# The short-convolution half of an output projection as block products, placed inside the SSD half

## The chip, the core and the metric

One NeuronCore of a Trainium2 chip runs one launch of the kernel. The metric is the device time of that launch in microseconds. PE is the matrix engine TensorE, DVE the vector engine, ACT the scalar engine, POOL GpSimd, and SP the sync engine, whose queue issues most transfers. SBUF is the on-chip memory, PSUM the accumulators that PE writes.

## The reference, cut to what matters

One layer of a hybrid decoder runs on 1024 prompt tokens and 8 x 8 sample tokens (1088 tokens in all, 1024 channels, float32). One input projection feeds a short gated convolution and a Mamba-2 scan (SSD). Both results, side by side, go through one output projection:

```python
h = rmsnorm(x, g_mix_pre) * (1 + scale_m) + shift_m
proj = h @ w_in
u = sc_c * sc_x
uc, new_sc_buf = causal_dwconv(u, sc_buf, sc_conv_w)
y_sc = sc_b * uc                       # 1024 channels
...
y_ssd = rmsnorm(yg, 1.0).reshape(bsz, L, SSM_WIDTH) * ssm_norm_g   # 1024 channels
mix = jnp.concatenate([y_sc, y_ssd], axis=-1) @ w_out              # 2048 x 1024
x = x + gate_m * rmsnorm(mix, g_mix_post)
h2 = rmsnorm(x, g_ffn_pre) * (1 + scale_f) + shift_f
f = (jax.nn.silu(h2 @ w_gate) * (h2 @ w_up)) @ w_down
x = x + gate_f * rmsnorm(f, g_ffn_post)
```

The change concerns the product of `y_sc` with the first 1024 rows of `w_out`, the "short-convolution half"; the product of `y_ssd` with the other 1024 rows is the "SSD half".

## The kernel before, in words

**Arithmetic.** A float32 value is held as a high part (`hi`, a cast on ACT) and a low part (`lo`, the difference, on DVE). A product of two such values is three matmuls: weight high with data high, weight high with data low, weight low with data high. In *plain* form (`acc3`, L343 to L345) a tile of 128 output channels takes 8 blocks of 128 input channels x 3 = 24 matmuls per chunk of tokens. The chunks `OC` of the output projection are 512, 304 and 272 tokens wide.

**Block products.** Much of the kernel uses a 2x2x2 scheme with seven products in place of eight (`unit`, L1085 on). Input channels, output channels and tokens are each cut in two. `combos_w` makes seven sums of weight blocks, `sums_h` seven of data blocks (the *factors*); each product p multiplies one with the other. A unit is two tiles of output channels over all 1088 tokens: for each product in the order 1, 5, 6, 3, 7, 2, 4 (`ORDER`) and for each token half q, 4 blocks x 3 = 12 matmuls of 272 columns (`product`, L1087 to L1089). A unit therefore has 7 x 2 x 12 = 168 matmuls, gathered in PSUM banks of the pools `pm` and `pz`, four banks each. After each product ACT copies the bank to its place or DVE adds it there.

**The short convolution's stage** (about 505 to 766 us) comes last in the mixer's input part. For each of 4 pairs of channel tiles there are three units (`sc_unit`), the convolution and the gating product. The pair's result `y_sc` is split whole (`split`, casts at L307) and written by SP to `y_d[0..7]` in device memory (L958, L959). `y_d[8..15]` hold the SSD result.

**The output projection** (from 765.72) has weights two tiles of output channels at a time (`load_cols`: raw transfer, cast L320, low half L321), two buffers of each part. First the SSD half: 8 tiles x 3 chunks, copied from PSUM into the accumulator `acc` by ACT. Then the short-convolution half plain: chunk 0 for all 8 tiles, chunk 1, and chunk 2, each added by DVE (L1330). Within chunk 1, at tiles 0, 2 and 5, stand the steps of `mix_tail` for tokens 0 to 511: transposes of `acc` back to rows (L1248), their scaling and statistics (L1250, L1255), an inverse root from short DVE operations (L282 to L294), the row update (L1265), and the second norm's statistics. After two tiles of chunk 2 the scaled rows (L1357, ACT) are transposed (L1365) as operands of the feed-forward part. The rest of chunk 2 is interleaved with that part's start.

**What sets the order.** A recording layer lays down each engine's instructions; `in_order` pins a piece behind the last recorded matmul, so in these stages PE runs tiles in the order of the code, and each engine works through its own queue in order.

## Time and profile before

| | |
|---|---|
| time, three runs | 1719.84, 1723.9, 1725.52 us (median 1723.9) |
| profiled execution | 1722.96 us, its span 1721.3 us, mean granted PE clock 0.992 |
| busy: PE, DVE, ACT, POOL | 97%, 67%, 45%, 11% of the span |
| last unit of the short convolution | 744.69 to 765.72 us |
| output projection up to the transposes at L1365 | 765.72 to 946.66 us |
| PE waits in 765 to 947 us | two: 2.3 us and 1.0 us |
| moved by transfers over the execution | 256.37 MB, mean 149 GB/s |

In a row of a timeline stand the start, the time from the start to the end, engine, line, operation, output and inputs, shapes, and in brackets the engine's idle time before it with what ended that. Consecutive matmuls overlap, so their distance from start to start is their pace, and their "busy" time is longer than that. In a row of windows stand the window, its busy time of PE, of PE's weight loads, DVE, ACT and POOL with counts, then the granted PE clock, the share of the transfer engines in use and GB/s.

### The profile page before, as it was taken

The numbers are of one execution on the slowest core, as the hardware profiler recorded it, in microseconds if no ns is written. First come the engines' busy times: TensorE is split into PE (matmuls) and PEld (weight loads), VectorE is DVE, ScalarE is ACT, GpSimd is POOL, SyncE is SP. The second block draws the span as 40 slices with busy tenths as digits, with TensorE's granted clock in tenths as the row PEclk, the third lists the DMA queues.
The fourth block names the chain that finished last, engine by engine and source line by source line (L and its number), as shares of the span: only waits on it lengthen the run. The fifth ranks groups of instructions, "written<-read, shape, count | busy, mean of one in ns | idle before, by whom it ended". The sixth has DMA issues, their size and how long they took to land. (4 is left out here: it accounts for less than half of the span.)

```text
span 1721.3 us, 31266 instructions
## 1 busy us (share of the span) xinstructions
PE 1676.9 (97%) x12604; PEld 1595.7 (93%) x12604; DVE 1145.5 (67%) x2190; ACT 772.1 (45%) x1575; POOL 185.5 (11%) x271
## 2 busy tenths in 40 slices
PE   5999999999999999999999999999999999999997
PEld 4898888899999999998989999999999999999987
DVE  5588777777798776661037879666665658688734
ACT  3447454557444433322226776444444446422222
POOL 2110101000001000000000000122222200022112
PEclk9999999999999999999999999999999999999999
DMA  9301344442412522348285634334434338865523
GB/s 318 79 13 38 120 147 155 150 127 77 131 48 79 176 83 62 114 164 305 69 257 184 196 135 147 115 141 142 145 135 141 140 117 314 320 244 197 201 92 139
DMA packets 159623, 256.37 MB, mean 149 GB/s; under 512 B 10577, under 2 KB 123393, under 8 KB 157942
## 3 DMA queue, kind: packets, MB, share of 16 engines
q1 hardware_dynamic: 159190, 253.19, 43.3%
q8 instruction: 99, 1.62, 0.4%
q10 hardware_dynamic: 288, 1.18, 0.2%
q14 instruction: 46, 0.38, 0.1%
HBM read 184.63 MB, written 69.71 MB: 148 GB/s over the span
## 5 line engine op out<-in xcount | busy, mean ns | idle before, releaser
L321 DVE TENSOR_TENSOR wl<-raw,wh 128x512 fp32r<-128x512 f32 (+1 forms) x87 | 61.2, 730 | 101.2 <-ACT wh L320 87.0
L343 PE MATMUL pm<-h,wh 128*128 128x384 f32 (+1 forms) x342 | 114.3, 334 | 0.0
L344 PE MATMUL pm<-h,wh 128*128 128x384 f32 (+1 forms) x342 | 114.0, 333 | 0.0
L345 PE MATMUL pm<-h,wl 128*128 128x384 f32 (+1 forms) x342 | 113.6, 333 | 0.0
L345 PE MATMUL pm<-hb,wl 128*128 128x512 f32 (+2 forms) x320 | 107.6, 338 | 2.3 <-DVE wl L321 2.3
L344 PE MATMUL pm<-hb,wh 128*128 128x512 f32 (+2 forms) x320 | 107.6, 337 | 0.0
L320 ACT CAST wh<-raw 128x512 fp32r<-128x512 f32 (+1 forms) x89 | 56.4, 666 | 114.0 <-PE pm L344 66.4
L343 PE MATMUL pm<-hb,wh 128*128 128x512 f32 (+2 forms) x320 | 105.6, 337 | 1.0 <-ACT wh L320 1.0
L1048 ACT CAST wd<-raw 128x256 fp32r<-128x256 f32 x112 | 42.9, 406 | 90.5 <-PE pz L1089 33.7
L345 PEld LDWEIGHTS pm<-hb,wl 128*128 128x128 f32 x320 | 60.9, 190 | 7.8 <-DVE wl L321 2.5
L1049 DVE TENSOR_TENSOR fs<-f,fs 128x576 fp32r<-128x576 f32 (+2 forms) x76 | 52.5, 705 | 21.6 <-ACT fs L1048 20.8
L343 PEld LDWEIGHTS pm<-hb,wh 128*128 128x128 f32 x320 | 60.6, 191 | 6.7 <-ACT wh L320 1.2
L343 PEld LDWEIGHTS pm<-h,wh 128*128 128x128 f32 x342 | 65.0, 190 | 1.5 <-issue 0.9
L344 PEld LDWEIGHTS pm<-h,wh 128*128 128x128 f32 x342 | 65.0, 190 | 1.2 <-issue 0.7
L1089 PE MATMUL pz<-fc,wd 128*128 128x288 f32 x224 | 66.2, 295 | 0.0
L1087 PE MATMUL pz<-fc,wd 128*128 128x288 f32 x224 | 66.2, 295 | 0.0
L1088 PE MATMUL pz<-fc,wd 128*128 128x288 f32 x224 | 66.1, 295 | 0.0
L345 PEld LDWEIGHTS pm<-h,wl 128*128 128x128 f32 x342 | 64.9, 190 | 1.2 <-issue 1.0
L344 PEld LDWEIGHTS pm<-hb,wh 128*128 128x128 f32 x320 | 60.8, 190 | 5.2
L1089 PE MATMUL pm<-fc,wd 128*128 128x256 f32 x224 | 63.2, 282 | 0.0
L1087 PE MATMUL pm<-fc,wd 128*128 128x256 f32 x224 | 63.1, 282 | 0.0
L1088 PE MATMUL pm<-fc,wd 128*128 128x256 f32 x224 | 62.9, 281 | 0.0
(5573 smaller groups left out, 6196.7 us busy)
## 6 DMA issues: line engine op xcount, KB each, us to landing
raw<-in_w_in SPq DMA_DIRECT2D x48, 512.0 KB
wa<-in_w_ada SPq DMA_DIRECT2D x32, 512.0 KB
raw<-in_w_out SPq DMA_DIRECT2D x32, 512.0 KB
f_d<-fs SPq DMA_DIRECT2D x28, 576.0 KB
f_d<-fs SPq DMA_DIRECT2D x30, 512.0 KB
raw<-in_w_gate SPq DMA_DIRECT2D x28, 512.0 KB
raw<-in_w_up SPq DMA_DIRECT2D x28, 512.0 KB
y_d<-y SPq DMA_DIRECT2D x26, 544.0 KB
```

The source lines that it names most:

```text
L320: (nc.gpsimd.tensor_copy if hi_eng else nc.scalar.copy)(wh, raw)
L321: (eng or nc.vector).tensor_tensor(wl, raw, wh, op=sub)
L343: mm(ps[:, :n], wh, xh, start=(first and j == 0), stop=False)
L344: mm(ps[:, :n], wh, xl, start=False, stop=False)
L345: mm(ps[:, :n], wl, xh, start=False, stop=(last and j == end))
L1048: nc.scalar.copy(hi, v)
L1049: (eng or nc.vector).tensor_tensor(lo, v, hi, op=sub)
L1087: mm(ps, W[0][k], X[0][k], start=(start and k == 0), stop=False, skip_group_check=True)
L1088: mm(ps, W[0][k], X[1][k], start=False, stop=False, skip_group_check=True)
L1089: mm(ps, W[1][k], X[0][k], start=False, stop=(stop and k == nk - 1), skip_group_check=True)
```

## The change

The short-convolution half of the output projection becomes four units of seven products over all 1088 tokens: 672 matmuls of 272 columns in place of 576 of 512, 304 and 272. The order of the stage is now: SSD half chunk 0 (opens the accumulator of the first 512 tokens, by ACT copies), the four units (their block that crosses token 512 is added on one side of it and opens the accumulator on the other, `acc_blocks`), SSD half chunk 1 with the tail of tokens 0 to 511, a small state output that stood earlier, SSD half chunk 2.

`y_sc` is no longer split and written whole. `factors` makes the seven data factors of a pair, by four DVE subtractions in place and a cast and a low half each. For the first three pairs that happens during the next pair's units, one step per product (`puts`): make a factor in the one buffer of the pool `psx`, then at the next step write it to `yx_d` with a transfer that ACT's queue issues. The last pair's factors are made during SSD chunk 0 and stay in SBUF, but for 2 and 4, which go through device memory. During chunk 0 SP's queue loads the others back; factors 2 and 4 of all pairs come last, into the slots of chunk 0's operands.

The SSD weights are now prepared by `plain_w` in eight slots, two pairs of tiles ahead, and the units' weights by `combos_w` in the same slots.

```diff
-    y_d = [drp.tile([P, 2, T], F32, tag=f"y_d{k}", name=f"y_d{k}") for k in range(16)]
+    y_d = [drp.tile([P, 2, T], F32, tag=f"y_d{k}", name=f"y_d{k}") for k in range(8)]
+    yx_d = [[drp.tile([P, 2, T // 2], F32, tag=f"yx_d{g}{p}", name=f"yx_d{g}_{p}") for p in range(1, 8)] for g in range(4)]
...
+    def factors(y, put):
+        (b11, b12), (b21, b22) = blocks_h(y[0]), blocks_h(y[1])
+        yield from put(1, b11)
+        yield from put(2, b21)
+        yield from put(3, b22)
+        nc.vector.tensor_tensor(b11, b12, b11, op=sub)
+        yield from put(5, b11)
+        nc.vector.tensor_tensor(b12, b22, b12, op=sub)
+        yield from put(7, b12)
+        nc.vector.tensor_tensor(b22, b22, b11, op=sub)
+        yield from put(6, b22)
+        nc.vector.tensor_tensor(b21, b21, b22, op=sub)
+        yield from put(4, b21)
+    def factor_parts(t, b):
+        t = t.bitcast(F32R).rearrange("p (s q n) -> p s q n", s=2, q=2)
+        part(t[:, 0], t[:, 1], b)
+    def put_sc(pr):
+        def put(p, b):
+            t = yt(psx)
+            factor_parts(t, b)
+            yield
+            nc.scalar.dma_start(yx_d[pr][p - 1].rearrange("p s n -> p (s n)"), t)
+            yield
+        return put
...
         for m in range(2):
-            y, hi, lo = cc[m], ext[m][:, :T].bitcast(F32R), cb[m].bitcast(F32R)
-            nc.vector.tensor_tensor(y, y, cb[m], op=mult)
-            split(hi, lo, y)
-            kept.append((2 * pr + m, hi, lo))
+            nc.vector.tensor_tensor(cc[m], cc[m], cb[m], op=mult)
         if pr < 3:
-            while kept:
-                y_out(*kept.pop(0))
+            puts = factors(cc, put_sc(pr))
...
-    rawp, wp = pool(left, "rawo", 4), pool(left, "wo", 2)
-    fa, fx, fb = pool(left, "fa", 4), pool(left, "fx", 8), pool(left, "fb", 7)
+    rawo, wo, fa = pool(left, "rawo", 4), pool(left, "wo", 4), pool(left, "fa", 4)
+    fx, fb = pool(left, "fx", 8), pool(left, "fb", 7)
+    raw_from, w_from = [rawo] * 4, [wo] * 4 + [fa] * 4
...
+    last = factors(y_last, put_last)
+    loads_ = (((1, 0), (1, 1), (1, 2), (5, 0), (5, 1), (5, 2)), ((6, 0), (6, 1), (6, 2)),
+              ((7, 0), (7, 1), (3, 0), (3, 1)), ((3, 2), (7, 2)))
+    for mp in range(4):
+        ws = out_load(mp)
+        load_factors(*loads_[mp])
...
+        for m in range(2):
+            in_order(out_tile, 0, terms0, ws[m], 2 * mp + m, True)
+            if mp < 2:
+                in_order(next, last, None)
+                in_order(next, last, None)
+    run(last)
+    load_factors(*((p, pr) for p in (2, 4) for pr in range(4)))
...
+    for mp in range(4):
+        W = combos_w(w_out, 0, nc.vector, raws_of.pop(0))
...
+        unit(W, X_o, 4, [0, 1], acc_blocks(mp), True, {}, SQ)
...
-    out_proj(0, terms[0], {0: [nxt], 2: [nxt]}, out_load)
-    tail = mix_tail([0, 1, 2, 3], lambda t: load_x(t, fb, "fm"), rows_fm, G_m)
+    terms = {c: out_split(c) for c in (1, 2)}
+    tail = mix_tail([0, 1, 2, 3], lambda t: load_x(t, fx, "fm"), rows_fm, G_m)
     out_proj(1, terms[1], {0: [tail], 2: [tail], 5: [tail]}, out_load)
+    in_order(conv_state, nsc, 8, 2, o["scc_p"], o["scc_s"], lambda: fx.tile([P, D], F32, tag="fm", name=nm("cs")))
     out_proj(2, terms[2], {1: [tail], 2: [tail]}, out_load, (0, 1))
```

Lines shift by two in the helpers: what was L343 to L345 is L345 to L347, L1087 to L1089 is L1089 to L1091, L1049 is L1051.

PE where the short-convolution half begins. Before, the last plain tile of the SSD half (272 columns) is followed by that half's chunk 0 (`hb` is a data operand, `wh` and `wl` the weight's parts):

```order
L343 MATMUL pm_975_8944<-hb_923_8229,wh_968_8808 128x272
L344 MATMUL pm_975_8944<-hb_924_8230,wh_968_8808 128x272
L345 MATMUL pm_975_8944<-hb_923_8229,wl_969_8809 128x272
L343 MATMUL pm_992_9006<-hb_978_8974,wh_988_8994 128x512
L344 MATMUL pm_992_9006<-hb_978_8974,wh_988_8994 128x512
L345 MATMUL pm_992_9006<-hb_978_8974,wl_989_8995 128x512
```

After, the last tile of the SSD half's chunk 0 is followed by product 1 of the first unit (`yx` is a factor read back):

```order
L345 MATMUL pm_995_8630<-hb_941_8325,wp__989_8593 128x512
L346 MATMUL pm_995_8630<-hb_941_8325,wp__989_8593 128x512
L347 MATMUL pm_995_8630<-hb_941_8325,wp__989_8593 128x512
L1089 MATMUL pm_1013_8701<-yx_948_8341,w1__1004_8672 128x272
L1090 MATMUL pm_1013_8701<-yx_948_8341,w1__1004_8672 128x272
L1091 MATMUL pm_1013_8701<-yx_948_8341,w1__1004_8672 128x272
```

Where the plain half had 24 groups (8 tiles in 3 chunks) of 24 matmuls, there are 28 products of 24 matmuls (two token halves of 12).

ACT's queue in the third pair of the short convolution, before (`w5` to `w7` are weight factors, the copies empty PSUM, L307 is the whole split):

```order
L1102 COPY y_840_7266<-pm_850_7296 128x272
L307 CAST y_837_7239<-y_797_6771 128x1088
L1102 COPY y_840_7266<-pz_851_7310 128x272
L1048 CAST w2__866_7517<-raw_861_7500 128x512
L1102 COPY y_856_7494<-pm_869_7527 128x272
L307 CAST y_838_7252<-y_798_6772 128x1088
L1102 COPY y_856_7494<-pz_870_7541 128x272
```

After, in the last pair, which makes the third's factors (128x544) and issues their writes:

```order
L1050 CAST y_892_7788<-y_804_6807 128x544
L1234 DMA yx_d2_5_134<-y_892_7788 128x1088
L1050 CAST w2__899_7810<-raw_894_7793 128x512
L1106 COPY y_871_7555<-pm_883_7587 128x272
L1050 CAST y_906_7878<-y_804_6807 128x544
L1106 COPY y_871_7555<-pz_884_7601 128x272
L1050 CAST w3__900_7814<-raw_894_7793 128x512
L1234 DMA yx_d2_7_136<-y_906_7878 128x1088
L1106 COPY y_872_7556<-pm_902_7820 128x272
```

Casts of half the width with their writes stand between the copies; the second cast shown uses the buffer that the first write reads.

DVE behind the row update in chunk 1, before (`wl_1076` and `wl_1078` are the low halves of the weights of tiles 6 and 7 of the same chunk, used by `pm_1079` and `pm_1080`):

```order
L1265 SCALAR_TENSOR_TENSOR x_1040_9338<-y_1044_9343,sm_1062_9471,x_1040_9338 128x1024
L1330 TENSOR_TENSOR acc1_8210<-acc1_8210,pm_1070_9538 128x304
L1330 TENSOR_TENSOR acc1_8210<-acc1_8210,pm_1071_9564 128x304
L321 TENSOR_TENSOR wl_1076_9612<-raw_1073_9607,wh_1075_9611 128x512
L321 TENSOR_TENSOR wl_1076_9612<-raw_1074_9609,wh_1075_9611 128x512
L282 TENSOR_SCALAR sm_1072_9590<-ssn_285 128x4
L321 TENSOR_TENSOR wl_1078_9618<-raw_1073_9607,wh_1077_9617 128x512
```

After (`wp__1130` and the two behind it belong to the first tiles of chunk 2, used by `pm_1134` and `pm_1135`):

```order
L1294 SCALAR_TENSOR_TENSOR x_1086_9632<-y_1090_9637,sm_1106_9761,x_1086_9632 128x1024
L1354 TENSOR_TENSOR acc1_8298<-acc1_8298,pm_1114_9828 128x304
L1354 TENSOR_TENSOR acc1_8298<-acc1_8298,pm_1115_9854 128x304
L1051 TENSOR_TENSOR wp__1130_9984<-raw_1128_9980,wp__1130_9984 128x512
L284 TENSOR_SCALAR sm_1116_9880<-ssn_305 128x4
L1051 TENSOR_TENSOR wp__1131_9987<-raw_1129_9982,wp__1131_9987 128x512
L291 TENSOR_SCALAR sm_1116_9880<-sm_1116_9880 128x4
L1051 TENSOR_TENSOR wp__1132_9990<-raw_1128_9980,wp__1132_9990 128x512
```

The weights' low halves at this place are those of a later pair of tiles. From the row update to the last of the short operations (L294, then L296) ten such low halves stand before, seven after.

More of the change, by code (lines that the diff above doesn't have):

```diff
@@ L1100, in unit @@
                 queue(product, ps, W[p], X[q][p], nk, new, p in (3, 2, 4))
-                if first and opens:
-                    nc.scalar.copy(out(q, i, h), ps)
-                else:
-                    nc.vector.tensor_tensor(out(q, i, h), out(q, i, h), ps, op=add)
+                to = out(q, i, h)
+                for v, cols, opening in to if isinstance(to, list) else [(to, slice(0, blocks_[q][1]), first)]:
+                    if opening and opens:
+                        nc.scalar.copy(v, ps[:, cols])
+                    else:
+                        nc.vector.tensor_tensor(v, v, ps[:, cols], op=add)
             for gen in between.get(n, ()):
@@ L1329, in out_tile, with out_load @@
         v = acc_at(m, c0, n)
-        nc.vector.tensor_tensor(v, v, ps[:, :n], op=add)
+        if opens:
+            nc.scalar.copy(v, ps[:, :n])
+        else:
+            nc.vector.tensor_tensor(v, v, ps[:, :n], op=add)
+    def out_load(mp):
+        W = plain_w(w_ssd, 256 * mp, raws_ahead.pop(0) if raws_ahead else None)
+        return [[[W[m, j][e][k] for j in range(2) for k in range(4)] for e in range(2)] for m in range(2)]
+    raws_ahead = [raws_plain(0), raws_plain(1)]
+    terms0 = out_split(0)
@@ new lines, in hymba_step, with x_tile, load_factors, put_last @@
+    staged = {p: yt(yp4) for p in (2, 4)}
+    x_tiles = {}
+    def x_tile(p, pr):
+        pl = {1: btp, 5: h2p, 6: fb, 3: yp4, 7: yp2 if pr == 2 else fb, 2: fx, 4: fx}[p]
+        t = x_tiles[p, pr] = yt(pl) if pl in (yp4, yp2) else pl.tile(
+            [P, T], F32, tag="bt" if pl is btp else "fm", name=nm("yx"))
+        return t
+    def load_factors(*which):
+        for p, pr in which:
+            nc.sync.dma_start(x_tile(p, pr), yx_d[pr][p - 1].rearrange("p s n -> p (s n)"))
+    def put_last(p, b):
+        t = staged[p] if p in staged else x_tile(p, 3)
+        factor_parts(t, b)
+        if p in staged:
+            nc.sync.dma_start(yx_d[3][p - 1].rearrange("p s n -> p (s n)"), t)
+        yield
@@ L1411, in out_load2 @@
     def out_load2(mp):
-        raws = [raw_half(w_out, j, 256 * mp) for j in range(2)]
+        raws = [raw_half(w_ssd, j, 256 * mp) for j in range(2)]
         out = []
```

83 lines of the change are left out of this document (41 added, 42 removed).

## The prediction

> **What bounds the kernel now.** I read the page's busy shares, its clock row and its chain of waits first, then where TensorE (PE) waited in the two stages the change touches, and last the timeline of each wait.
>
> ```profile
> span 1721.3 us, 31266 instructions
> PE 1676.9 (97%) x12604; PEld 1595.7 (93%) x12604; DVE 1145.5 (67%) x2190; ACT 772.1 (45%) x1575; POOL 185.5 (11%) x271
> PEclk9999999999999999999999999999999999999999
> PE 34%; issue 4%; DVE 2%; ACT 1%; DMA 1%; POOL 1%; SPq 0%; POOLq 0%; DVEq 0%; ACTq 0%
> ```
>
> PE is busy 97% of the span at nearly full clock, and no other engine comes near. So a time follows from how long PE streams and where it stands still. The profiled execution took 1722.96 us (span 1721.3), 0.94 us under the median of 1723.9; the sum below is made against 1722.96.
>
> A matmul's busy time overlaps the next one's, so its price is start to start. The timeline of PE, first the short convolution's last unit and the first tile of the output projection, then chunk 0 of its short-convolution half:
>
> ```profile
> 744.69 0.29 PE L1087 MATMUL pm<-bt,w__896_7964 128*128 128x272 f32 x1
> ...
> 765.72 0.40 PE L343 MATMUL pm<-hb,wh 128*128 128x512 f32 x1
> ...
> 767.11 0.40 PE L343 MATMUL pm<-hb,wh 128*128 128x512 f32 x1
> ...
> 901.78 0.39 PE L343 MATMUL pm<-hb,wh 128*128 128x512 f32 x1
> ...
> 903.14 0.39 PE L343 MATMUL pm<-hb,wh 128*128 128x512 f32 x1
> ```
>
> From the unit's first matmul (744.69) to the first of the projection (765.72) are 21.03 us for 7 products x 2 token halves x 12 = 168 matmuls: **0.1252 us** per 272 columns. Six matmuls of 512 columns take 1.39 us in the SSD half, 0.2317 each, and 1.36 us in the other half, 0.2267.
>
> Where PE waited between 765 and 947 us is two rows; the timeline shows both and what came after the longer one:
>
> ```profile
> PE pm L345 <- DVE wl L321: 2.3, 1, 2.3
> PE pm L343 <- ACT wh L320: 1.0, 1, 1.0
> ```
> ```profile
> 790.71 0.50 PE L343 MATMUL pm<-hb,wh 128*128 128x512 f32 x1 [0.99 <-ACT wh L320]
> ...
> 932.63 0.41 PE L345 MATMUL pm<-hb,wl 128*128 128x304 f32 x1 [2.30 <-DVE wl L321]
> 932.88 0.30 PE L343 MATMUL pm<-hb,wh 128*128 128x304 f32 x1
> ...
> 933.71 0.30 PE L343 MATMUL pm<-hb,wh 128*128 128x304 f32 x1
> ...
> 934.02 0.46 PE L345 MATMUL pm<-hb,wl 128*128 128x304 f32 x1
> ...
> 937.32 0.31 PE L343 MATMUL pm<-hb,wh 128*128 128x304 f32 x1
> ...
> 946.66 0.71 PE L1365 MATMUL pz<-ident,x 128*128 128x128 f32 x5
> ```
>
> A 304-column matmul takes 0.138 us (six from 932.88 to 933.71). After the 2.30 us wait, the thirteen from 934.02 to 937.32 took 3.30 us, 0.254 each: PE ran at half pace and lost 3.30 - 13 x 0.138 = 1.5 us more. 946.66 is the first transpose of the finished rows (line L1365); up to it the projection took 946.66 - 765.72 = 180.9 us.
>
> **The change, part by part.** *Products.* The short-convolution half now is 8 tiles x 24 matmuls in each chunk: 192 x (0.2267 + 0.138 + 0.1252) = 94.1 us (all 24 matmuls of one tile counted, the last six tiles of chunk 2 beyond 946.66 included). After the change it is four units of 168 matmuls of 272 columns, lines, shapes and order of operands those of the unit above: 4 x 21.03 = 84.1 us. **Gain 10.0 us.** All of it lies on PE, so it counts in full unless a wait fills it. The SSD half keeps its 576 matmuls; if its opening tiles and others swapped the two paces of 512, this would be 192 x 0.005 = 1.0 us either way.
>
> *The wait for the weights' low half.* Vector engine (DVE) and scalar engine (ACT) rows around it:
>
> ```profile
> 926.34 4.88 DVE L1265 SCALAR_TENSOR_TENSOR x<-y,sm,x 128x1024 f32<-128x1024 f32 x4
> 931.13 0.85 DVE L1330 TENSOR_TENSOR acc<-acc,pm 128x304 f32<-128x304 f32 x2
> 931.89 1.29 DVE L321 TENSOR_TENSOR wl<-raw,wh 128x512 fp32r<-128x512 f32 x2
> ...
> 940.88 0.47 DVE L1330 TENSOR_TENSOR acc<-acc,pm 128x304 f32<-128x304 f32 x1
> 941.26 0.16 DVE L294 SCALAR_TENSOR_TENSOR sm<-sm 128x4 f32<-128x4 f32 x1
> ```
> ```profile
> 941.77 4.27 ACT L1357 ACTIVATE x<-x,sm 128x1024 f32<-128x1024 f32 x4
> ```
>
> The low halves of tile 6's weights (931.89) stand in DVE's queue behind 4.88 us of row updates. In the changed order the low halves at this place belong to the next chunk's first tiles; those of tile 6 stand ahead of the row updates. **The 2.30 and the 1.5 go, 3.8 us.** What is late next would be the scaled rows that the transposes at 946.66 read. DVE's statistics end with L294 (941.26), just after the sum of chunk 1's last tile (940.88); ACT then needs until 941.77 + 4.27 = 946.04, so 5.2 us from that sum. PE has two chunk-2 tiles meanwhile (48 x 0.125 = 6.0 us), and the change puts the small state output between, which adds to the 6.0. That chain follows PE's tile, so it moves forward with it: I cost it at nothing. Should DVE lag instead, the chain keeps its old length; that is rival B.
>
> *The wait for the high half* (1.0 us, at 790.71) came where weights are one pair ahead; with eight slots they are two: **1.0 us**, or nothing if ACT is late for another reason.
>
> *Sums.* 10.0 + 3.8 + 1.0 = 14.8 us. New waits cost some of it; bounds follow.
>
> *Factors in the short convolution's stage.* Per pair of channel tiles the whole split (two casts and two low halves of 1088 columns) becomes seven of 544, with four subtractions. At 0.72 us per 544 columns DVE gets 7 + 4 - 4 of them more, 5.0 us per pair of 63 us (three units). Beside:
>
> ```profile
> L1049 DVE TENSOR_TENSOR h<-t,h x2: 723/724/725, 509.2 to 514.2; 128x544 fp32r<-128x544 f32 x2
> PE pm L1089 <- DVE w__680_5277 L1049: 1.3, 1, 1.3
> 650.00:700.00 50.00, 50.00 (x404) 49.94 (x403) 30.93 (x54) 16.06 (x34) 2.74 (x6) 1.00 0.17 48
> 700.00:748.00 48.00, 48.00 (x386) 48.00 (x385) 33.41 (x54) 19.06 (x39) 3.01 (x8) 1.00 0.26 91
> ```
>
> In these windows (PE, PE loads, DVE, ACT, POOL) DVE is busy 62 to 70% and ACT 32 to 40%; 5 us in 63 add 8 points to DVE. PE covers it; the bound from above is the 1.3 us that a unit's late weight low half cost once, so 0 to 4 us for three pairs. I take 0.3.
>
> *The write of each factor.* One buffer holds a factor until its transfer has landed; the next factor's cast waits in ACT's queue for that, and behind it stand the copies that empty PSUM. The nearest rows, a write of about this size and the cast that waits for it, and a like wait in the FFN:
>
> ```profile
> 538.04 0.34 SPq L958 DMA_DIRECT2D y_d<-y  x1
> ```
> ```profile
> 542.17 1.11 ACT L307 CAST y<-y 128x1088 fp32r<-128x1088 f32 x1 [2.15 <-DMA y_d<-y]
> ...
> 1306.31 1.37 ACT L1048 CAST fs<-f 128x576 fp32r<-128x576 f32 x2 [4.07 <-DMA f_d<-fs]
> ```
>
> Landing takes 542.17 - 538.04 = 4.1 us; a product step (24 matmuls) is 3.0 us. So a cast that comes one step after the issue blocks ACT about 1.1 us, 20 times. PSUM has eight banks and a unit holds six accumulators, which lets ACT lag some 1.5 steps, 4.5 us, before PE stands. PE shows no wait beside either row. Cost 0; bound 20 x 1.1 = 22 us if none were hidden.
>
> [...]
>
> *Loads.* The projection's start:
>
> ```profile
> 766.00:780.00 14.00, 14.00 (x76) 12.15 (x75) 4.79 (x5) 2.36 (x4) 0.00 (x0) 1.00 1.03 381
> 780.00:800.00 20.00, 19.01 (x121) 17.52 (x121) 2.50 (x4) 4.86 (x11) 0.00 (x0) 1.00 0.89 307
> 800.00:820.00 20.00, 20.00 (x119) 17.95 (x119) 2.77 (x4) 4.15 (x9) 0.00 (x0) 1.00 0.76 284
> ```
>
> Last columns: DMA share and GB/s. Factors read back are 28 x 0.557 MB = 15.6 MB, where 8.9 MB of whole rows were read later. Their first product comes after chunk 0, at 765.7 + 192 x 0.2317 = 810.2. The last eight (2 and 4, 4.5 MB) take the slots of chunk 0's operands, free from about 805; their products are sixth and seventh, at 810.2 + 15.0 and + 18.0. At 284 GB/s 4.5 MB take 15.7 us, at 381 11.7: done by 817 to 821 when nothing else is ahead. Cost 0 to 0.5. The next chunk's operands take slots that products 5 and 6 free 12 to 15 us before a unit's end; nothing.
>
> I allow 0.5 us for all borders: 14.8 - 0.3 - 0.5 = **14.0 us**, 1709.0 in the profiled execution's frame; the median is 0.94 higher, but a second execution's wobble is larger, so I stay with **1709**.
>
> **The rivals.**
>
> *B: the tail of tokens 0 to 511 takes the stall's place.* For: DVE worked nearly without a break from 919 to 941. Against: three of its ten weight low halves leave that stretch, and its end follows PE's tile. Price: the 3.8 us come back, 1713. [...] If the slow stretch has another cause and stays, 1.5 us are not saved, 1710.5, inside A's range.
>
> *C: loads and weights come late at the borders.* For: queues at 1.03 of their share in 766:780, and one SP queue that carries factors, weights and the last pair's two staged writes in order, so that one blocked issue holds all behind it. Against: 5 to 12 us of slack above. Price: 6.7 MB more at 381 GB/s are 17.6 us if all stand open, 1726; half, 1718.
>
> *D, the other side: ACT blocked by the single factor buffer.* If landing is slower than 4.1 us beside the weight loads, the lag grows over the seven factors; from 4.5 us of lag PE waits for PSUM in the short-convolution stage. Fully open 22 us, less the 14 gained: 1731; with the low half's 0.7 us ahead of each issue added, 1745. Against: ACT has 60% of its time free.
>
> That the products are not replaced is excluded by the order of instructions: 672 stand where 576 stood.
>
> **How the numbers follow.** A 0.60 (1705 to 1712), B 0.12 (1712 to 1714), C 0.18 (1713 to 1727), D 0.10 (1726 to 1745). A measurement of this kernel tells 0.3%, 5.2 us, from no change: faster is below 1718.7, slower above 1729.1. Faster: A, B and 0.09 of C, 0.81. Same: 0.08 of C and 0.01 of D, 0.09. Slower: 0.01 of C and 0.09 of D, 0.10. The range 1703 to 1719 holds A, B and half of C; 1705 to 1712 is A's own.
>
> **What would show it.** Products: PE starts of 0.125 us through four stretches of 21.0 us where the plain half stood, and about 167 us instead of 180.9 from the projection's first matmul to the first L1365-like transpose. Stall: no wait of PE for a low half in chunk 1, full pace there. B: a wait of PE for ACT's scaled rows. C: PE waiting for a DMA, or for a cast whose source landed late, near 810 to 828. D: ACT's factor casts with idle time of over 3 us released by DMA, and PE waiting for ACT's copies between 560 and 765. The prediction is wrong if the short-convolution stage grows by over 4 us, or if the units' pace is not 0.125.

## The result and the profile after

The changed kernel takes **1712.1 us**, the median of five runs (1706.52 to 1713.61), where the kernel before took 1725.52 beside it (five runs, 1719.84 to 1728.46). The ratio is **0.9922, with a 95% interval of 0.9905 to 0.9938**: 13.4 us faster, between 10.7 and 16.4. The forecast was 1709.0 in a range of 1703 to 1719, faster by 14.0.

The page of the changed kernel, its span and busy times:

```profile
span 1710.4 us, 31655 instructions
...
PE 1667.0 (97%) x12700; PEld 1593.2 (93%) x12700; DVE 1194.1 (70%) x2294; ACT 788.0 (46%) x1615; POOL 187.1 (11%) x271
```

PE streams 9.9 us less and bounds the kernel as before. The timeline of PE at the borders of the new order, each row a start and a length:

```profile
744.01 0.29 PE L1089 MATMUL pm<-bt,w__917_8056 128*128 128x272 f32 x1
...
765.04 0.40 PE L345 MATMUL pm<-hb,wp__944_8329 128*128 128x512 f32 x1
...
808.61 0.29 PE L1089 MATMUL pm<-yx,w__1004_8672 128*128 128x272 f32 x1
...
892.56 0.30 PE L345 MATMUL pm<-hb,wp__1078_9588 128*128 128x304 f32 x1
...
929.78 0.27 PE L1452 MATMUL pz<-ident,x 128*128 128x128 f32 x1
```

The last short-convolution unit still takes 765.04 - 744.01 = 21.03 us. Chunk 0 of the SSD half takes 808.61 - 765.04 = 43.57. The four new units take 892.56 - 808.61 = **83.95 us for 672 matmuls**, 0.1249 each. From the projection's first matmul to the first transpose of the finished rows are 929.78 - 765.04 = **164.74 us** in place of 180.9. In all of 744 to 960 us the view of waits names none for PE.

The start of the kernel varies: the first short-convolution unit began between 494 and 505 us in the profiles of this study. So the runs are compared below by stages, each the distance between PE starts in one profile: the short-convolution stage (its first unit to the projection's first matmul), the projection (to the transposes of its rows), the feed-forward part (to the first matmul of the down projection), and the rest (to PE's end).

| profile | SC stage | projection | feed-forward | rest |
|---|---|---|---|---|
| before | 266.56 | 180.94 | 512.55 | 253.07 |
| before, second profile | 266.55 | 180.89 | 513.44 | 253.10 |
| after | 266.57 | 164.74 | 516.93 | 254.22 |
| after, second profile | 266.55 | 164.74 | 516.29 | 255.17 |

The projection gained 16.2 us, more than forecast; the feed-forward part, whose instructions the change does not touch, **gave back 3 to 4.4**, and the rest 1 to 2. The stages together say 10.7 and 11.2 us. The windows of the feed-forward part, before and after (PE, PE loads, DVE, ACT, POOL, each busy us with counts; clock; transfer share; GB/s):

```profile
946.66:1459.20 512.54, 507.88 (x4026) 505.06 (x4025) 355.99 (x617) 271.16 (x529) 71.56 (x73) 1.00 0.45 154
```
```profile
929.78:1446.70 516.92, 509.13 (x4026) 505.13 (x4025) 355.73 (x616) 269.67 (x529) 72.64 (x73) 1.00 0.45 154
```

The same 4026 matmuls at the same clock, but PE stands idle 516.92 - 509.13 = 7.8 us where it was 512.54 - 507.88 = 4.7: 3.1 of the 4.4 us. The other 1.2 stand as longer busy time. The waits of PE from 1000 to 1500 us show new entries, first before, then after (engine, line, releaser: us in total, times, longest):

```profile
PE pz L1089 <- DVE w__1267_11174 L1049: 0.7, 1, 0.7
PE pz L1087 <- DVE f L1104: 0.7, 1, 0.7
```
```profile
PE pz L1089 <- ACT sg L1106: 1.4, 2, 0.9
PE pz L1089 <- DVE f L1108: 1.1, 1, 1.1
PE pz L1091 <- DVE w__1314_11479 L1051: 0.7, 1, 0.7
```

With the smaller ones left out they add up to 2.0 us before and 4.3 after. This loss is what most of the experiments below look for.

### The profile page after: what moved, and what is told of

It is laid out like the page before. It is cut to its first block, busy times and chain, and to the rows that moved or that the text cites. A ratio compares the mean times of both kernels' runs of the same rounds, so it can differ in the third digit from the quotient of the medians.

```text
span 1710.4 us, 31655 instructions
## 1 busy us (share of the span) xinstructions
PE 1667.0 (97%) x12700; PEld 1593.2 (93%) x12700; DVE 1194.1 (70%) x2294; ACT 788.0 (46%) x1615; POOL 187.1 (11%) x271
## 3 DMA queue, kind: packets, MB, share of 16 engines
q8 instruction: 100, 1.64, 0.4%
## 5 line engine op out<-in xcount | busy, mean ns | idle before, releaser
L345 PE MATMUL pm<-h,wh 128*128 128x384 f32 (+1 forms) x342 | 114.5, 335 | 0.0
L347 PE MATMUL pm<-h,wl 128*128 128x384 f32 (+1 forms) x342 | 113.7, 333 | 0.0
L1051 DVE TENSOR_TENSOR fs<-f,fs 128x576 fp32r<-128x576 f32 (+2 forms) x76 | 52.5, 703 | 28.2 <-ACT fs L1050 27.7
L345 PEld LDWEIGHTS pm<-h,wh 128*128 128x128 f32 x342 | 65.1, 190 | 1.8 <-issue 0.9
L1089 PE MATMUL pz<-fc,wd 128*128 128x288 f32 x224 | 66.1, 295 | 0.0
L1091 PE MATMUL pz<-fc,wd 128*128 128x288 f32 x224 | 66.1, 295 | 0.0
L347 PEld LDWEIGHTS pm<-h,wl 128*128 128x128 f32 x342 | 64.9, 190 | 1.2 <-issue 1.0
L1050 ACT CAST fs<-f 128x576 fp32r<-128x576 f32 (+2 forms) x76 | 44.5, 600 | 45.9 <-DMA f_d<-fs 27.8
L1091 PE MATMUL pm<-fc,wd 128*128 128x256 f32 x224 | 63.2, 282 | 0.3 <-DVE wd L1051 0.3
L1089 PE MATMUL pm<-fc,wd 128*128 128x256 f32 x224 | 63.1, 282 | 0.3 <-ACT wd L1050 0.3
L1051 DVE TENSOR_TENSOR wd<-raw,wd 128x256 fp32r<-128x256 f32 x112 | 53.1, 482 | 11.3 <-ACT wd L1050 10.7
L1108 DVE TENSOR_TENSOR facc<-facc,pz 128x288 f32<-128x288 f32 x96 | 43.1, 449 | 12.4 <-PE pz L1091 12.4
L1108 DVE TENSOR_TENSOR facc<-facc,pm 128x256 f32<-128x256 f32 x96 | 39.8, 414 | 13.7 <-PE pm L1091 12.2
L1846 DVE TENSOR_TENSOR facc<-facc,pm 128x512 f32<-128x512 f32 (+2 forms) x24 | 12.7, 532 | 51.3 <-PE pm L347 51.3
L345 PE MATMUL pm<-ff,wd 128*128 128x512 f32 (+2 forms) x144 | 48.2, 334 | 0.0
L347 PE MATMUL pm<-ff,wd 128*128 128x512 f32 (+2 forms) x144 | 47.9, 333 | 0.0
L346 PE MATMUL pm<-ff,wd 128*128 128x512 f32 (+2 forms) x144 | 47.9, 333 | 0.0
```

The costliest lines, as they stand in the source:

```text
L345: mm(ps[:, :n], wh, xh, start=(first and j == 0), stop=False)
L346: mm(ps[:, :n], wh, xl, start=False, stop=False)
L347: mm(ps[:, :n], wl, xh, start=False, stop=(last and j == end))
L1050: nc.scalar.copy(hi, v)
L1051: (eng or nc.vector).tensor_tensor(lo, v, hi, op=sub)
L1089: mm(ps, W[0][k], X[0][k], start=(start and k == 0), stop=False, skip_group_check=True)
```

## The experiments

**1. The changed kernel once more, unaltered.** Does the loss in the feed-forward part belong to the change or to one execution?

> The changed kernel once more, unaltered. The first profile of it showed the projection 16.2 us shorter up to the transposes at L1452, and then 1.1 us lost at 964.6 us (PE waits for DVE, L1279), 1.9 us between 1041 and 1063 and 2.4 us between 1428 and 1471 (PE waits for casts and copies on ACT that stood behind a write's landing). If these later losses belong to the change, they stand at the same places again with about the same sizes, and the ratio to the kernel before is again 0.992 (about 13 us). If those from 1041 on are chance of one execution, they are absent or elsewhere here, and the profile then ends about 15 us under that of before; the 1.1 us at 964.6 should come back in either case.

Measured: 1709.51 us, ratio 0.9922 [0.9908, 0.9936], six runs. The waits for `sg`, `f` and the weights between 1000 and 1500 us are there again, with two short ones for transfers (0.7 and 0.4 us), and all add up to 4.45 us; the feed-forward part took 516.29. The wait for `tl` at L1277, just behind the projection, was 0.4 us here and 1.0 in the first profile, and most later profiles lack it: that one wanders. The others come with the change.

**2. SSD weights one pair of tiles ahead.** Only the number of slots that the plain weights use is set back, from eight to four:

```diff
-    def plain_w(w, cols, raws=None):
+    def plain_w(w, cols, raws=None, pools=None):
...
-                t = in_turn(w_from).tile([P, 2, 4, P], F32R, tag="wc", name=nm("wp_"))
+                t = in_turn(pools or w_from).tile([P, 2, 4, P], F32R, tag="wc", name=nm("wp_"))
...
-        W = plain_w(w_ssd, 256 * mp, raws_ahead.pop(0) if raws_ahead else None)
+        W = plain_w(w_ssd, 256 * mp, raws_ahead.pop(0) if raws_ahead else None, [wo] * 4)
```

> The changed kernel, with the SSD weights of the projection prepared one pair of tiles ahead (four slots) in place of two. Theory: the gain of waits (2.30 + 1.5 us at tile 6 of chunk 1) comes from the weights' low halves standing ahead of the row update; undone, PE waits again 2 to 3.5 us for DVE at that tile, and the time is 2.5 to 5 us over the changed kernel's. Rival: the wait vanished because the stage is laid out anew or DVE has less to do; then PE does not wait there and the time is within 1 us of the changed kernel's.

Measured: 1713.66 us, ratio 0.9946 [0.9933, 0.9959], four runs; the projection took 167.83 us, 3.1 more. The waits of PE in it:

```profile
PE pm L347 <- DVE wp__1119_9901 L1051: 1.7, 1, 1.7
...
```

The wait for tile 6's low half returns, 1.7 us of the 2.3 and without half pace behind it; the two left out are of 0.3 us each. In the changed kernel the timeline of DVE has that low half 7.8 us ahead of the row updates:

```profile
904.26 0.69 DVE L1051 TENSOR_TENSOR wp__1119_9901<-raw,wp__1119_9901 128x512 fp32r<-128x512 f32 x1
...
912.02 4.87 DVE L1294 SCALAR_TENSOR_TENSOR x<-y,sm,x 128x1024 f32<-128x1024 f32 x4
```

So it is the second pair in hand that removes the stall, not the new place of the chunk.

**3. The stall alone taken out of the kernel before.** In it, the low halves of tiles 6 and 7 of chunk 1 go from DVE to POOL; still one pair is ahead:

```diff
-    out_proj(1, terms[1], {0: [tail], 2: [tail], 5: [tail]}, out_load)
+    out_proj(1, terms[1], {0: [tail], 2: [tail], 5: [tail]},
+             lambda mp: out_load(mp, nc.gpsimd if mp == 3 else None))
```

> The kernel before, with the low halves of the weights of tiles 6 and 7 in chunk 1 of the short-convolution half made by POOL in place of DVE, nothing else changed. Theory: PE's wait of 2.30 us and the half pace after it (1.5 us) are worth 3.8 us, and nothing takes their place at once: the projection up to the transposes at L1365 takes 177.1 us in place of 180.9. Rival: the chain of row statistics takes the place (PE waits up to 3.8 us at the transposes) and the stretch stays above 180 us; or the half pace stays without the wait, and 1.5 us of the 3.8 remain.

Measured: 1724.54 us, ratio 1.0 [0.9991, 1.0009], ten runs; the projection took 183.05 us, 2.1 *more*. The waits of PE in it:

```profile
PE pm L343 <- ACT wh L320: 3.1, 3, 1.7
PE pm L345 <- DVE wl L321: 0.8, 2, 0.6
PE pm L345 <- POOL wl L321: 0.8, 1, 0.8
```

The 2.3 us are gone and others stand in their place, with half pace behind the last of them (granted clock 0.50 from 941.70 to 945.11 us, so on into the transposes). One of these waits, 0.8 us for POOL's low half, is made by the edit itself, so the run does not price the late operation alone. One pair ahead is one tile pair's time for raw transfer, cast and subtraction; that each small delay in it comes out on PE is argued from these waits and not shown by itself. The 3.8 us of the forecast came with eight slots; taking away the one late operation in this way did not bring them.

**4. Factors written at once.** The pause between making a factor and writing it is taken out, so the single buffer comes free a step earlier:

```diff
             factor_parts(t, b)
-            yield
             nc.scalar.dma_start(yx_d[pr][p - 1].rearrange("p s n -> p (s n)"), t)
```

> The changed kernel, with each factor's write issued in the same step as its cast, so that the next factor follows one product step (3.0 us) later and no longer two; still one buffer. In the changed kernel ACT waited 13.5 us in all for these landings, 3.6 us at most, and PE never waited for ACT there. A factor's cycle is now cast 0.65 us, low half 0.72 us and landing some 3 to 4.6 us, 5 us or more against a step of 3.0, so ACT falls behind by 2 us or more with each of seven factors. Theory (PSUM covers some 4.5 us of ACT's lag): ACT waits 2 to 3 times as long for landings, PE begins to wait for ACT's copies in each of the three pairs, and the time is 3 to 25 us over the changed kernel's. Rival: ACT catches up between factors because it is idle half the time, PE still does not wait, and the time is within 2 us.

Measured: 1707.53 us, ratio 0.9921 [0.9906, 0.9937], four runs. ACT's waits for the landing of a factor, in the changed kernel and in this one:

```profile
ACT y L1050 <- DMA yx_d<-y: 13.5, 11, 3.5
```
```profile
ACT y L1050 <- DMA yx_d<-y: 12.6, 11, 3.6
```

The waits hardly change, and neither do the starts of the factors' casts: within a pair they stand 4.1 to 7.6 us apart in both kernels. So the pause did not set that distance, and this run loads the buffer no more than the changed kernel does. None of these waits reaches PE in either kernel. (The short-convolution stage took 267.94 us here, 1.4 more, but with the granted clock at 0.50 from 507.24 to 510.65 us, before the first factor is made.) ACT blocked by the single buffer is real, 13.5 us in all, and free.

**5. The landing doubled.** After each factor's write POOL's queue reads it back into its buffer, so the buffer is held for a second transfer:

```diff
             nc.scalar.dma_start(yx_d[pr][p - 1].rearrange("p s n -> p (s n)"), t)
+            nc.gpsimd.dma_start(t, yx_d[pr][p - 1].rearrange("p s n -> p (s n)"))
             yield
```

> The changed kernel, with each factor's write followed by a transfer that reads the same factor back into the one buffer (POOL's queue), so that the buffer is free only after a second landing; the data stay the same. A factor's cycle on ACT becomes cast 0.65 + low half 0.72 + two landings of 3 to 4.6 us, 8 to 10 us, against the 6.0 us (two product steps) that PE takes per factor. Theory (rival D's mechanism, with PSUM covering some 4.5 us of lag): ACT waits 3 to 5 us per factor, falls behind by 2 to 4 us with each, and PE waits for ACT's copies: 10 to 18 us per pair, 30 to 50 us in all, and the time is above that of the kernel before. Rival: ACT's other idle time takes it up, PE does not wait, and the time stays within 3 us of the changed kernel's.

Measured: 1730.7 us, ratio 1.0043 [1.0026, 1.006], six runs; the short-convolution stage took 280.72 us (14.2 more) and the projection 171.80 (7.1 more). ACT's waits and then PE's:

```profile
ACT y L1050 <- DMA y<-yx_d: 48.2, 16, 8.0
```
```profile
PE pm L1091 <- DVE w__860_7365 L1051: 4.0, 1, 4.0
PE pm L345 <- DMA hb<-y_d: 3.7, 5, 1.8
PE pm L1089 <- ACT w__796_6618 L1050: 2.6, 1, 2.6
PE pm L1091 <- DVE w__796_6618 L1051: 2.2, 1, 2.2
PE pm L1089 <- ACT y L1106: 0.2, 1, 0.2
```

With waits of up to 8.0 us ACT's queue does stop PE: the mechanism of rival D exists. But PE waits for weights. The cast of `w__796` stands behind a factor's cast in ACT's queue; the low half of `w__860` stands in DVE's queue behind a factor's low half, which waits for that factor's cast. The waits for PSUM copies (L1106), which D named, come to 0.2 us. The cover is the weights' lead. These waits make 9.0 of the stage's 14.2 us; behind them the granted clock is 0.50 from 628.09 to 634.91 and from 696.35 to 703.18 us.

**6. The small state output on POOL's queue.** Its two staged writes (`conv_state`, moved by the change) now stand on SP's queue ahead of the feed-forward part's first weight loads. Is that why the wait at L1277 is new? They go to POOL's queue:

```diff
-            nc.sync.dma_start(o_p[0, 0][:, cols], stg[:k, :])
-            nc.sync.dma_start(o_s[0].rearrange("b k c -> (b k) c")[:, cols], stg[k:, :])
+            (q_ or nc.sync).dma_start(o_p[0, 0][:, cols], stg[:k, :])
+            (q_ or nc.sync).dma_start(o_s[0].rearrange("b k c -> (b k) c")[:, cols], stg[k:, :])
...
-    in_order(conv_state, nsc, 8, 2, o["scc_p"], o["scc_s"], lambda: fx.tile([P, D], F32, tag="fm", name=nm("cs")))
+    in_order(conv_state, nsc, 8, 2, o["scc_p"], o["scc_s"], lambda: fx.tile([P, D], F32, tag="fm", name=nm("cs")), nc.gpsimd)
```

> The changed kernel, with the two writes of the short convolution's new state issued by POOL's queue and no longer by SP's. In the changed kernel they sat on SP's queue ahead of the first loads of the gate weights, which were issued 2 us after the transposes at L1452 began, where before they were issued 6.6 us ahead of them. Theory A: this makes the casts of the gate weights and what follows on ACT late and causes the 1.1 us wait at 964.6; then that wait goes, and perhaps some of those between 1041 and 1063: 1 to 3 us less than the changed kernel. Theory B: the late issue has slack; then the first gate weights are loaded some 8 us earlier, and the wait at 964.6 stays within 0.3 us.

Measured: 1709.16 us, ratio 0.9916 [0.9903, 0.9928], five runs. The first load of the gate weights on SP's queue, in the changed kernel with a write ahead of it, and here; then PE's wait here:

```profile
928.94 0.28 SPq L1126 DMA_DIRECT2D out_scc_p<-cs  x1
...
931.73 1.00 SPq L1046 DMA_DIRECT2D raw<-in_w_gate  x2
```
```profile
927.79 0.97 SPq L1046 DMA_DIRECT2D raw<-in_w_gate  x2
```
```profile
PE pz L1277 <- DVE tl L1279: 1.5, 1, 1.5
```

The load is issued 1.95 us behind the first transpose in the changed kernel (at 929.78) and 1.95 us behind it here (at 925.84). So the writes ahead of it do not hold it; something else does, which was not looked for. The wait stays, at 1.5 us, the projection at 164.74 and the feed-forward part at 517.59: the order on SP's queue is not the cause.

**7. The kernel before once more.** A profile to set beside experiment 1.

> The kernel before once more, unaltered, for a second profile: whether its waits for landings of f_d stay at 2.7 us or less before 1180 us and its waits of PE between 1000 and 1500 us at 2 us in all (systematic), or come out at the 4 us of the changed kernel's profiles (chance of an execution). The wait of 2.3 us at tile 6 of chunk 1 should be there again.

Measured: 1719.77 us. The 2.3 us stall is there again, the waits of PE from 1000 to 1500 us add up to 1.5 us, and the feed-forward part took 513.44. The loss is therefore a difference between the kernels, 3 to 4.4 us.

A part of the spread within each kernel is the clock. Near the start of this stage PE waits some 2 us for the scaled rows (L1365, L1452) in every profile. Behind that wait the granted clock is 0.50 for 3.41 us in this profile (986.74 to 990.15 us) and in those of experiments 1, 2, 4, 6, 9, 10 and 12, and stays at 1.00 in the others. So like goes with like: 512.55 us with 516.93 at full clock, 513.44 with 516.29 with the slow stretch.

The loss was followed to one place. Behind the waits near its start both kernels run the feed-forward part in step until ACT casts a factor whose buffer waits for the write of the one before. The row of that cast, the same instruction, before and after:

```profile
1043.95 0.63 ACT L1048 CAST fs<-f 128x512 fp32r<-128x512 f32 x1 [2.69 <-DMA f_d<-fs]
```
```profile
1030.56 0.62 ACT L1050 CAST fs<-f 128x512 fp32r<-128x512 f32 x1 [4.90 <-DMA f_d<-fs]
```

From the issue of the write to the cast are 2.74 to 2.76 us in four profiles with the instructions of the kernel before (experiments 3 and 8 among them), and 4.0 to 5.0 in all eight of the changed kernel and its variants up to experiment 10. The write has 0.52 MB in both. Two causes remained: the place of the buffer `f_d` in device memory, which the change moved, and something else in the transfer engines.

**8 to 10. The place in device memory.** In the kernel before, `y_d` is padded so that `f_d` lies where the changed kernel has it (26.34 MB); in the changed one it is padded until `f_d` lies elsewhere (29.12 MB):

```diff
-    y_d = [drp.tile([P, 2, T], F32, tag=f"y_d{k}", name=f"y_d{k}") for k in range(16)]
+    y_d = [drp.tile([P, 2, T + (236, 240)[k % 2]], F32, tag=f"y_d{k}", name=f"y_d{k}")[:, :, :T] for k in range(16)]
```

> The kernel before, with unused columns behind each y_d tensor in device memory, so that f_d begins at 26.34 MB as in the changed kernel and no longer at 22.44 MB; no instruction is added or moved. (The run that was to move f_d in the changed kernel left it at 26.34 MB, since places are given out by first use; it is a repetition of the changed kernel.) Theory: the place of f_d sets how long its writes take to land; then ACT's wait near 1041 us becomes 4 to 5 us in place of 2.7, PE waits 4 us in place of 2 between 1000 and 1500 us, and from the transposes at L1365 to the down projection it takes 2 to 4 us more than 513 us. Rival: nothing changes there.

Measured: 1722.38 us, ratio 0.9993 [0.9979, 1.0007], ten runs; the cast waited 2.71 us and the feed-forward part took 512.08, as before.

```diff
-    y_d = [drp.tile([P, 2, T], F32, tag=f"y_d{k}", name=f"y_d{k}") for k in range(8)]
+    y_d = [drp.tile([P, 2, T + 340], F32, tag=f"y_d{k}", name=f"y_d{k}")[:, :, :T] for k in range(8)]
```

> The changed kernel with unused columns behind each y_d tensor, so that f_d begins at 29.12 MB; no instruction is added or moved. Theory (place in device memory): the waits for f_d's landing change with the third place. Rival (the place means nothing): ACT's first wait for f_d stays at 4.0 to 4.9 us and the stretch from the transposes at L1452 to the down projection at 514.6 to 517.6 us, as in the profiles so far.

Measured: 1709.07 us, ratio 0.992 [0.9901, 0.9938], four runs; the cast waited 4.32 us and the part took 515.29. The place does not account for this wait: it is 2.69 us in the kernel before and 2.71 with `f_d` moved there, 4.90 in the changed kernel and 4.32 with `f_d` moved here.

A third run declared sixteen of the factor buffers ahead of `f_d` and twelve behind it:

```diff
-    yx_d = [[drp.tile([P, 2, T // 2], F32, tag=f"yx_d{g}{p}", name=f"yx_d{g}_{p}") for p in range(1, 8)] for g in range(4)]
+    yx_of = lambda n: [drp.tile([P, 2, T // 2], F32, tag=f"yx_d{j}", name=f"yx_d{j}") for j in n]
+    yx_ = yx_of(range(16))
...
+    yx_ += yx_of(range(16, 28))
+    yx_d = [yx_[7 * g:7 * g + 7] for g in range(4)]
```

> The changed kernel, with the same tensors in device memory in another order: 16 of the 28 factor tensors ahead of the feed-forward's f_d, 12 behind, so that f_d lies as far from the start as in the kernel before. No instruction is changed. In four profiles of kernels of the changed layout ACT waits 4.6 to 5.0 us for a write of f_d (in the feed-forward's first third), where two of the old layout show 2.7 us or less at the same instructions, and PE then loses 2 to 4 us up to 1480 us. Theory: the place of f_d in device memory sets how long its writes take to land; then the waits return to 2.7 us and the feed-forward is 2 to 3 us shorter. Rival: the place means nothing, and these waits stay at 4.5 us or more.

Measured: 1709.78 us, ratio 0.9934 [0.992, 0.9948], six runs. The buffers of this program lay by first use and not by declaration, so `f_d` stayed at 26.34 MB: this run told nothing of the place and counts as a repetition. The cast waited 3.96 us, the part took 514.59.

**11. The count of PE's instructions.** The transfer queues in the window from the write's issue to the cast that waits for it (packets, MB, share of 16 engines), before and after:

```profile
q1 hardware_dynamic: 144, 0.52, 43.0%
```
```profile
q1 hardware_dynamic: 144, 0.52, 26.9%
q8 instruction: 1, 0.02, 2.4%
```

In the changed kernel one packet of instructions shares the window; 2.4% of 16 engines over 4.9 us are 1.9 us of one engine. The page of the changed kernel's profile lists 100 such packets with 1.64 MB, 16 KB each; in the short convolution's units they come about 16.1 us apart, the time of 128 matmuls of 0.125 us with their 128 weight loads. Over the whole execution the traces of the two kernels hold 25344 and 25546 instructions of PE (matmuls, weight loads, semaphore events) beside 99 and 100 packets, 256.0 and 255.5 to a packet. From these counts comes the estimate that the packets carry PE's instructions, 256 in each. How packet and write meet can be read from the times of the transfers. In the changed kernel the packet runs from 1026.48 us for 1.91 us, to 1028.39. Of the write's 144 packets 135 have begun by 1027.9 us. Nine, a sixteenth, are left, and they run one by one (window 1027.9:1030.1; the first row is in 40 slices, in which 75 is one packet of 4 KB):

```profile
GB/s 0 0 0 0 0 0 0 0 75 0 0 0 0 0 0 0 75 0 0 0 0 75 0 75 0 0 75 0 0 75 0 0 75 0 0 75 0 0 0 0
DMA packets 9, 0.03 MB, mean 15 GB/s; under 512 B 1, under 2 KB 1, under 8 KB 9
```

The first of them starts at 1028.38, as the instruction packet ends, the last at 1029.99, and the cast follows at 1030.56. Nine of 144 packets are what one of 16 engines would carry, so this is read as one engine's share of the write standing behind the packet, and the cast waiting for that share; no view names the engine of a packet.

The changed kernel lays 202 more PE instructions ahead of this place, so its packet falls elsewhere in the same work. If that is the cause, 54 instructions more make 256 and put the packet back. Added are 27 transposes near the kernel's start (a weight load and a matmul each) into a bank that nobody reads:

```diff
         nc.tensor.transpose(cps[:, k * 32:(k + 1) * 32], crow[:, k * P:(k + 1) * P], ident[:32, :32])
+    pad = pz()
+    for _ in range(27):
+        nc.tensor.transpose(pad[:, :32], crow[:, :P], ident[:32, :32])
```

> The changed kernel, with 27 small transposes added on PE near the start, where PE waits for its first rows (9 to 13.6 us); their result is not used. PE's instructions are fetched in blocks of 16 KB, one packet some 16 us after the other (128 matmuls with their weight loads). In the three profiles of the kernel before the first awaited write of f_d lands 2.7 us after its issue and no such packet lies between; in three of the changed kernel's layout one of 1.4 to 1.9 us does, and the cast behind it waits 4.4 to 5.0 us. The change adds 202 instructions to PE's stream ahead of that place (counted in the traces), 54 fewer than a block; 54 more put the fetches back where the kernel before had them. Theory (the fetch delays the one of sixteen shares of the write that lies behind it): the cast waits 2.7 us again, PE waits 2 us in place of 4 between 1000 and 1500 us, and from the transposes at L1452 to the down projection it takes 512 to 514 us in place of 514.6 to 517.6; the time falls by 2 to 4 us against the changed kernel's. Rival: the overlap is chance and these numbers stay.

Measured: **1706.0 us, ratio 0.9898 [0.9881, 0.9915]**, four runs; the stages are 266.57, 164.74, **511.57** and 254.07. The cast's row, and the waits of PE from 1000 to 1500 us, in this kernel:

```profile
1026.32 0.62 ACT L1053 CAST fs<-f 128x512 fp32r<-128x512 f32 x1 [2.67 <-DMA f_d<-fs]
```
```profile
PE pz L1094 <- DVE w__1315_11507 L1054: 0.7, 1, 0.7
...
PE pz L1092 <- DVE f L1111: 0.2, 1, 0.2
```

The write's window holds no instruction packet, the cast waits as in the kernel before, the new waits of PE are gone (1.5 us in all) and with them the whole loss: 511.57 is below even the 512.55 before, both without the slow stretch of experiment 7. Matmul by matmul, the first profile of the changed kernel falls behind this one by 1.7 us up to 975 us (the wait for `tl` among them), by 2.3 from 1041 to 1064 and by 1.3 from 1428 to 1441. This kernel computes what the changed one does, with 54 useless instructions more. It is the fastest of this study; its interval meets that of the changed kernel (0.9881 to 0.9915 against 0.9905 to 0.9938), so the time alone does not settle that it is faster than it. The stage speaks for it, with one profile here: 511.57 us against 514.59 to 517.59 in the eight of the changed kernel and its variants.

**12. The same from the other side.** In the kernel before, 101 such transposes, 202 instructions, give PE's stream the alignment of the changed kernel:

```diff
+    pad = pz()
+    for _ in range(101):
+        nc.tensor.transpose(pad[:, :32], crow[:, :P], ident[:32, :32])
```

> The kernel before, with 101 such transposes near the start, their result not used: 202 instructions, so that PE's fetches fall in the feed-forward as in the changed kernel. The transposes themselves take some 10 us, of which about 4 lie in PE's first wait, so the whole time says nothing; what counts is the feed-forward. Theory: a fetch of 1.4 to 1.9 us now lies behind the write of f_d, the cast near 1040 us waits 4 to 5 us in place of 2.7, PE waits 3.5 to 4.5 us in place of 2 between 1000 and 1500 us, and from the transposes at L1365 to the down projection it takes 515 to 517.5 us in place of 512 to 513.5. Rival (the gain of the run before came from something else in the changed kernel): these numbers stay at 2.7, 2 and 513.

Measured, one run: 1731.17 us, of which the whole says nothing, since the transposes themselves hold up the start (the first unit at 504.7 us instead of 494 to 499). The window of the write, the cast's row and the first of PE's waits in the feed-forward part:

```profile
q1 hardware_dynamic: 144, 0.52, 32.6%
q8 instruction: 1, 0.02, 1.6%
```
```profile
1051.30 0.63 ACT L1051 CAST fs<-f 128x512 fp32r<-128x512 f32 x1 [3.91 <-DMA f_d<-fs]
```
```profile
PE pz L1090 <- DVE f L1107: 1.0, 1, 1.0
...
PE pz L1090 <- ACT sg L1105: 0.6, 1, 0.6
```

The packet appears, the cast waits 3.91 us, PE's waits add up to 3.4 us with the changed kernel's names in them (`sg`, `f`), and the part took 515.04: 1.6 us more than in experiment 7, which has the slow stretch too. So the alignment of PE's instruction stream makes this loss in either kernel, in one profile each. That it acts through the transfer engine which the packet shares with the write is read from the times of the transfers; no run moves the packet alone.

## Why the prediction was right, and where it was not

**Products: right.** 94.1 to 84.1 was forecast; the units took 83.95. All of the 10 us counted, since no wait filled them.

**The wait for the low half, 3.8 us: right, for the reason given.** Experiment 2 brings 1.7 of its 2.3 us back by slots alone. The forecast counted 1.5 us of half pace into it, with a doubt. The timeline of experiment 8, the padded kernel before, has the same stall, but full pace behind it:

```profile
928.97 0.41 PE L345 MATMUL pm<-hb,wl 128*128 128x304 f32 x1 [2.28 <-DVE wl L321]
929.21 0.30 PE L343 MATMUL pm<-hb,wh 128*128 128x304 f32 x1
...
930.87 0.30 PE L343 MATMUL pm<-hb,wh 128*128 128x304 f32 x1
```

Twelve matmuls from 929.21 to 930.87 took 0.138 us each, and the projection 179.35 us in place of 180.9. So the half pace may stay away at the same wait. The granted clock (the figure behind POOL's count) differs too. The stretch that holds the wait and the one behind it, in the kernel before and in experiment 8:

```profile
930.49:933.90 3.41, 1.27 (x9) 1.27 (x10) 3.41 (x9) 3.41 (x8) 0.13 (x1) 1.00 1.02 416
933.90:937.31 3.41, 3.41 (x15) 3.41 (x14) 2.05 (x7) 1.45 (x4) 0.00 (x0) 0.50 0.73 214
```
```profile
925.14:928.55 3.41, 1.54 (x12) 1.30 (x10) 3.41 (x6) 3.37 (x7) 0.13 (x1) 1.00 1.05 416
928.55:931.96 3.41, 2.99 (x21) 2.99 (x22) 3.41 (x10) 3.14 (x7) 0.00 (x0) 1.00 0.72 274
```

These stretches are those of the clock's record: in the kernel before it changes at 449.21, 456.04, 933.91 and 937.32 us, which are 2, 140 and 1 times 3.413 us apart. There nearly the whole wait fell into one of them (3.41 - 1.27 = 2.14 us without PE), and the next ran at 0.50. In experiment 8 the wait lies across the border at 928.55, with 1.87 us ahead of it, and the clock stayed at 1.00. Why the clock fell in the one and not in the other is not shown beyond this difference. So whether the 1.5 us are there to gain depends on the execution: the first two profiles of the kernel before and experiment 12 have them, experiment 8 does not. In the two profiles of the changed kernel the question does not arise, since PE does not wait there.

**The wait for the high half, 1.0 us: right.** It is gone.

**What was left open as 1.0 us either way came out as a gain.** Chunk 0 of the SSD half took 43.57 us for 192 matmuls, 0.2269 each, where the eight tiles of 512 took 44.6 us among narrower ones before: 1.0 us. With the products (10.15), the two waits (3.3) and the half pace (1.5) that makes 16.0 of the projection's 16.2.

**Factors, 0.3 us, and borders, 0.5: both measured nothing.** The short-convolution stage is 266.57 us against 266.56, with DVE at the higher load that was worked out. Three windows of the changed kernel, over stretches that the prediction quotes of before:

```profile
650.00:700.00 50.00, 50.00 (x404) 49.92 (x403) 35.39 (x62) 18.29 (x38) 2.80 (x6) 1.00 0.30 101
700.00:748.00 48.00, 48.00 (x385) 48.00 (x385) 37.88 (x63) 21.41 (x44) 2.79 (x9) 1.00 0.40 137
...
800.00:820.00 20.00, 20.00 (x131) 18.52 (x130) 13.07 (x23) 8.63 (x18) 0.00 (x0) 1.00 1.05 391
```

DVE goes from 62 and 70% to 71 and 79%, 9 points where 8 were estimated, and PE is busy throughout. At the loads' border (800 to 820) the transfers run at 391 GB/s and PE is not kept waiting, so **rival C** did not happen. **Rival B** did not either: PE does not wait ahead of the transposes, and its waits for the scaled rows of later tokens are the same in both kernels, first before, then after:

```profile
PE pz L1365 <- ACT x L1357: 2.5, 2, 2.1
```
```profile
PE pz L1452 <- ACT x L1444: 2.5, 2, 2.1
```

**Rival D** was there as a wait of ACT, 13.5 us against the bound of 22, and none of it reached PE. Its path was named wrongly: experiment 5 shows that what runs out first is the lead of the weights (three waits of PE, 8.8 us) and not PSUM (0.2 us). The 4.5 us of ACT's lag that PSUM was to cover were an estimate from this kernel's two pools of four banks, and no run shows that limit.

**What the prediction left out.** It stopped at the transposes and took the rest of the program as unchanged; the rest lost 3 to 4.4 us in the feed-forward part and 1 to 2 after it. The sum of 14.0 came near the medians' 13.4 because 16.2 were gained and some 5 given back, and that is luck; by the stages of the profiles the net is 10.7 to 11.2. By its number alone 1712.1 lies on the border of A's range and B's; it is the traces that show A's terms and nothing of B. The cause of the first loss is shown by experiments 11 and 12 to be the count of PE's instructions ahead of that place, but for the wandering wait for `tl` (up to 1.5 us), whose cause stays open. Open, too, is the loss of about 1 us after the first matmul of the down projection: with the instructions realigned it is still 254.07 against 253.07, and 253.23 in experiment 12. Experiment 8, a variant of the kernel before, has 253.89, so a part of it is chance of an execution.

## What to carry to other kernels

With PE busy 97% of the time, the 10.15 us of fewer columns through it counted in full here, since the operands stayed ahead; a second step of lead removed a whole family of small waits (without it the projection took 3.1 us more), while curing the one late operation only showed the next (2.1 us more). When a change alters the number of PE's instructions, look far behind it too: here the feed-forward part moved by 3.0 to 6.0 us with 54 instructions (experiment 11) and by 1.6 with 202 (experiment 12). So compare stage by stage, and try a few dozen useless instructions before looking for a cause in the changed code.

## What the runs showed of the hardware

- **A packet of instructions beside a write.** The profile of the changed kernel has 100 instruction packets of 16 KB, one for some 256 instructions of PE by the estimate of experiment 11. One ran beside a 0.52 MB write, to 1028.39 us, and the last sixteenth of the write's packets began only at 1028.38. The cast that waits for the write stood 3.9 to 4.9 us with such a packet in its window and 2.7 without (four profiles, experiments 11 and 12). No other wait was traced to a packet.
- **Two paces of 512 columns.** In the changed kernel's unbroken run of 192 such matmuls the first dozen came 0.231 us apart and the others 0.2267; where tiles of 512 alternated with narrower ones before, four tiles without a wait took 0.2314 to 0.2321 a matmul. No run shows why.
- **Stretches at half clock behind partly idle ones.** In the fourteen profiles, from 480 us on, each stretch of 3.41 us at full clock in which PE idled 1.9 us or more (twelve, 1.93 to 2.90 us) was followed by one at 0.50. None with 1.5 us or less was, and of nine between them four were. The wait of 2.3 us cost 1.5 us more in the kernel before, and nothing more in experiment 8, where it lay across a border.
